# Re-timed loads, broadcasts and a gate pair in a Strassen-Winograd gated decoder block on one core

## The chip, the cores and the metric

The kernel runs on one core of one Trainium2 chip, in one launch. The metric is the device time of that launch in microseconds (us). Three runs before the change took 1220.03, 1220.82 and 1221.76 us; the median is 1220.82 us.

## The reference, cut to what matters

One decoder layer for 2048 tokens of width 1024, all in float32:

```python
c_act = silu(c)
shift, scale, gate = split(c_act @ w_ada + b_ada, 3)       # modulation
h = rms(x, g_pre) * (1 + scale) + shift
q, k, v, z_a, u_b, v_b, z_b, g = split(h @ w_in, ...)      # 4864 columns
q, k = rope(q, positions), rope(k, positions)              # 8 q heads, 2 k heads of 64
y_a = window_attention(q, k, v, sinks) * silu(z_a)         # blocks of 128
y_b = gelu(u_b) * (w_s @ layernorm(gelu(v_b)) + b_s) * silu(z_b)   # chunks of 128
merged = sigmoid(g_a) * (y_a @ w_proj_a) + sigmoid(g_b) * (y_b @ w_proj_b)
x = x + gate * rms(merged @ w_out, g_post)
```

## The kernel before, in words

**Products.** The large matrix products are Strassen-Winograd products: seven half-size products (p = 0 to 6) instead of eight. Both operands are split into a high and a low part, so one half-size product is twelve matmuls of 128x512: for each of four slices of the contraction, high by high, high by low (of the tokens) and low by high (of the weights), in `mm3` (L163, the matmul is on L168). The high part of a weight tile is a cast on ScalarE (L216), the low part a subtraction on VectorE (L217, shown as L151 W). The sums of weight quarters that Winograd needs (S1 to S4) are made in `combos` (L243), by VectorE for the first four column blocks and by GpSimd (L154) for the others, and are stored to `sS` for the second half of the tokens. The sums of the first four blocks stand in a list `sums`, which `sum_to` works off; the sum with index 4 to 7 is S1 of block 0 to 3, index 8 to 11 is S2 of block 0 to 3.

**Steps.** One step (`step`, L229) is one such product, twelve matmuls, 2.72 us from start to start where nothing waits. `slot` counts the steps. `later(n, f)` puts f ahead of the step n steps on, with `True` behind it. Every engine works through its own instructions in the order in which the program emits them; the order is written out by hand (`manual_schedule`), so an instruction that waits holds up all that stands behind it on its engine. DMAs go through SP's queue, but for a few.

**Stages.** The tokens are cut into two halves (s = 0, 1). Of the 38 column blocks of 128 of `w_in`, each Winograd block takes two: 19 blocks of seven steps, 133 steps for each half. The order of the blocks is the list `kinds` (L1255), matched by the column order in `_layout` (L1489). In the first half the first four blocks run interleaved: step 4p + i is product p of block i (steps 0 to 27). Step 28 is the first of the fifth block. While the steps go on, hooks do the rest: `rope_finish` (L881) turns q and k by the rotation tables (two DMAs, a multiplication on GpSimd, three operations on VectorE, a cast, two stores), `ln_step` transposes and normalises v_b, `att_block` does one of 16 attention blocks, eight steps apart, `ev_uz` the spatial gating, and `y_step`, `o_step` and `presum` make sums for later stages (GpSimd). After the two halves, `Pair` (L434) makes both projections of the first token half for two feature blocks at once, with eight PSUM banks, then come the second half and the output product.

**The start.** The token operand of product p (`T[p]`) is made on the fly in `t_part` (L748). It needs the modulation (`ada_row`, 16 matmuls for each of eight rows in all, then `ada_rows_out`, `ada_fin`) and the reciprocal root of each token's mean square (`rstd`, L643), which `rstd_out` (L653) broadcasts over the partitions with eight short matmuls and a copy. `rope_steps` makes the 24 VectorE operations on the angles, `rope_out` (L610) the sine and cosine tables, which go to DRAM (`cs_s`). `load_rope` (L798) loads them from there into four tiles of the pool `m` (four buffers, of which two hold results of the interleaved blocks up to steps 20 and 21) with four DMAs for each table.

**PSUM.** Four banks X, Y, Z, W are fixed, two (`s`) are the two halves of one tile S, two (`b`) are handed out by `bank()`.

Of the kernel before, what the change touches and what calls it, by code (L numbers as in the profile page):

```python
# [55 lines left out]
def hybrid_block(ctx: ExitStack, tc: tile.TileContext, xt, x, wada, wgate, wI, wP, wO,  # L56
# [286 lines left out]
    for n in range(NPAIR - NLAST):  # L343
        stream_fresh(wI_quads(n), n)
        if n == NFIRST - 1:
            by_product(NFIRST)
    for n in range(NPAIR - NLAST, NPAIR):
        stream_stored(wI_quads(n), n)
    by_product(NLAST)
# [268 lines left out]
    def rope_do(n):  # L618
        for _ in range(n):
            next(rope_it, None)  # L620
# [66 lines left out]
    def ada_rows_out(hf):  # L687
        rows[hf, "sb"] = flat("e")
        act.copy(rows[hf, "sb"], rows[hf])
# [84 lines left out]
    low_now()  # L774
    ada_load(1)
    cur["cap"] = 3 * NFIRST - 1
    ada_rows_out(0)
    warm(1, 2)
    ada_fin(0)
# [9 lines left out]
    want(NFIRST - 1)  # L789
    square_sums(1)  # L790
    low_now()
    rope_do(26)
    rope_out()


    ropet = {}

    def load_rope(s):  # L798
        for h in range(2):
            g = 2 * s + h  # L800
            for i, key in enumerate("cs"):
                t = flat("m")
                for r in range(4):
                    at = 64 * (r // 2) + r % 2
                    sp.dma_start(t[at : at + 64 : 2, :] if at < 64 else t[at:P:2, :], cs_s[i][32 * g : 32 * (g + 1), :])
                if key == "s":
                    later(3, lambda t=t: act.activation(out=t, in_=t, func=AF.Copy, scale=col[:, C_SGN : C_SGN + 1]))
                ropet[key, h] = t

    def setup_sgu():  # L810
        sp.dma_start(wT, ws)
# [101 lines left out]
    def ev_kv(s):  # L913
        def ev(key, src, psum):
            h = half(key)
            if ft(key) == 0:
                def put_out(hi, lo):
                    ks = slice(P + s * NT + h * 512, P + s * NT + (h + 1) * 512)
                    for i, t in enumerate((hi, lo)):
                        sp.dma_start(k_s[:, i, ks], t)  # L920
                rope_finish(h, rope_in(src, psum, "e"), put_out, (9, 3)[h] if s == 0 else h)
            else:
                t = src
                if psum:
                    t = flat("e")
                    act.copy(t, src)

                def turn():
                    b = bank()
                    for c in range(4):  # L930
                        pe.transpose(b[:, c * P : (c + 1) * P], t[:, c * P : (c + 1) * P], ident)

                    def out_():
                        o = flat("qS"[s])
                        act.copy(o, b)
                        at = 1 + s * 8 + h * 4
                        store(1, v_s[:, at : at + 4, :], o.rearrange("p (a b) -> p a b", a=4))
                    later(1, out_)
                later((3, 10)[h] if s == 0 else 2, turn, True)
        return ev  # L940

    def ev_q(s, g0):
        def ev(key, src, psum):
            h, g = half(key), g0 + ft(key)

            def put_out(hi, lo):
                for i, t in enumerate((hi, lo)):
                    sp.dma_start(q_s[s][:, i, g, h * 512 : (h + 1) * 512], t)
            rope_finish(h, rope_in(src, psum, "x"), put_out, ("11", "22", "12", "21").index(key))
        return ev  # L950

    def silu2(src, dst, psum, then=None):
# [297 lines left out]
    def run_all():  # L1250
        nonlocal T

        for s in range(NS):
            uz = [{} for _ in range(4)]
            kinds = [lambda: ev_vb(s, 0), lambda: ev_vb(s, 2), lambda: ev_kv(s), lambda: ev_g(s, 0), lambda: ev_q(s, 0),  # L1255
                     lambda: ev_q(s, 2), lambda: ev_za(s, 0), lambda: ev_za(s, 2)]
            kinds += [lambda c=c: ev_uz(s, c, uz[c]) for c in range(4)]
            kinds += [lambda j=j: ev_g(s, j) for j in range(1, 8)]

            if s == 0:  # L1260
                later(24, setup_sgu)
                later(28, zero_heads)
            later((23, 12)[s], lambda s=s: load_rope(s))
            for i in range(8):
                later((27 + 5 * i // 2, 17 + 3 * i)[s], lambda i=i: ln_step(s, i))
            for c in range(4):
                later(52 + 7 * c, lambda c=c: uz_load(s, c, uz[c]))
            for i in range(8):
                for off, post, f in att_block(s * 8 + i):
                    later(62 + 8 * i + off, f, post)  # L1270
            if s == 0:
                for i in range(8):
                    later(30 + 5 * i, lambda i=i: h1_stats(i))
                later(71, h1_rstd)
                for kt in range(4):
                    later(76 + 10 * kt, lambda kt=kt: h1_step(kt))
                for i in range(NLAST):
                    later(91 + 10 * i, lambda i=i: presum(NPAIR - NLAST + i, wI_quads(NPAIR - NLAST + i)))
            else:
                for i in range(4):  # L1280
                    later((1, 57, 64, 71)[i], lambda i=i: y_step((2, 3, 0, 1)[i]))
                for i in range(2):
                    later((78, 83)[i], lambda i=i: presum(NPAIR + i, p_quads(2 + i)))
                for kk in range(KT):
                    later(30 + 7 * kk, lambda kk=kk: gate_step(kk))
                for h in range(2):
                    later((91, 98)[h], lambda h=h: gate_end(h))
                for kt in range(4):
                    later(94 + 6 * kt, lambda kt=kt: o_step(kt))

            n0 = 0
            if s == 0:
                n0 = NFIRST
                S = pS.tile([P, 2, 512], F32, tag="s", name=nm("s"))
                bX = bank()
                rows["bank"] = bank()
                bks = [two_banks(BK["X"], BK["W"]), two_banks(BK["Y"], BK["Z"]), two_banks(S[:, 0, :], S[:, 1, :]),
                       two_banks(bX, rows["bank"])]
                blks = [Block(bks[i], kinds[i](), "mmee"[i]) for i in range(NFIRST)]

                def second_half():
                    ada_row(1, range(2))
                    rstd_out(1, BK["W"])
                    sum_to(2 * NFIRST - 1)
                    want(NFIRST)
                    ada_row(1, range(2, 8))
# [52 lines left out]
        S = pS.tile([P, 2, 512], F32, tag="s", name=nm("s"))  # L1359
        c = S[:, 0, :], S[:, 1, :], bank(), bank()  # L1360
        for n in range(2):
            blk = Pair(n, (BK, {"X": c[0], "W": c[1], "Y": c[2], "Z": c[3]}))
            for p in range(7):
                w = w_get()
                step(lambda: blk.run(p, w, T))
# [99 lines left out]
def _layout(inputs):  # L1465
# [26 lines left out]
    for j in range(1, KT):  # L1492
# [55 lines left out]
```

## Time and profile before

| | |
|---|---|
| median of three runs | 1220.82 us |
| the profiled execution | 1221.22 us |
| its span | 1219.5 us |
| mean granted TensorE clock | 0.993 |
| TensorE matmul (PE) busy | 1191.7 us, 98% of the span |
| VectorE (DVE) busy | 866.4 us, 71% |
| ScalarE (ACT) busy | 631.9 us, 52% |
| GpSimd (POOL) busy | 345.4 us, 28% |

A timeline row gives the start, the duration, the engine and line, the operation, what it writes and reads, the count of merged instructions, and in brackets the idle time of the engine ahead of it and what ended it. Rows of a merged group start where the group starts. SPq is SP's queue; its rows are the issuing of DMAs, not the transfers. In a list of waits the three numbers are the total in us, how often, and the longest.

### The profile page before, as it was taken

What the parts mean: (1) busy time and instruction counts of PE and PEld (TensorE: products, weight loads), DVE (VectorE), ACT (ScalarE), POOL (GpSimd) and SP (SyncE); (2) the same over time, 40 slices, a digit from 0 to 9 for tenths busy, and PEclk for the clock granted to TensorE, in tenths of its full rate; (3) what the DMA queues carried; (4) which work ended last, traced back from release to release, by engine and by line L of the source; (5) the groups of instructions that cost most, each with busy time, mean ns of one, the idle gap of its engine ahead of it and who ended that gap; (6) DMA issues with size and microseconds to landing.
All of it is one profiled execution on the core that took longest, in us unless ns stands there. A gap on an engine that the chain in (4) does not pass through costs nothing.

```text
span 1219.5 us, 17353 instructions
## 1 busy us (share of the span) xinstructions
PE 1191.7 (98%) x5450; PEld 951.1 (78%) x5450; DVE 866.4 (71%) x1319; ACT 631.9 (52%) x1367; POOL 345.4 (28%) x290
## 2 busy tenths in 40 slices
PE   8999899999999999999999999999999999999997
PEld 3677687888777777888878787777777888888886
DVE  7888589567868667346876877654786877767775
ACT  4475345475766677443445665555854512444443
POOL 0001365233456301011402122321033301155443
PEclk9999999999999999999999999999999999999999
DMA  9536888959899998578799899889967988855452
GB/s 350 219 121 204 280 296 294 279 167 220 261 353 349 311 298 301 180 228 273 244 282 294 252 258 327 275 266 283 340 217 240 384 275 266 286 170 172 139 182 87
DMA packets 227972, 311.74 MB, mean 256 GB/s; under 512 B 20900, under 2 KB 102948, under 8 KB 227880
## 3 DMA queue, kind: packets, MB, share of 16 engines
q1 hardware_dynamic: 227408, 309.94, 78.9%
q8 instruction: 43, 0.70, 0.2%
q0 software_dynamic: 176, 0.53, 0.2%
q14 instruction: 49, 0.40, 0.1%
q10 hardware_dynamic: 296, 0.16, 0.1%
HBM read 200.77 MB, written 104.53 MB: 250 GB/s over the span
## 4 chain that ended last, share of the span: by engine, by line
PE 89%; DVE 6%; ACT 2%; issue 2%; POOL 1%; DMA 0%; SPq 0%; DVEq 0%; POOLq 0%; ACTq 0%
PE bankY L168 28%; PE bankX L168 19%; PE bankZ L168 12%; PE bankW L168 12%; PE b L168 4%; PE s L168 4%; PE b L1095 2%; PE s L1045 2%; PE s L1046 1%; PE b L984 1%; DVE W L151 1%; PE b L1080 1%; PE b L683 1%; DVE e L157 1%; PE b L863 0%
## 5 line engine op out<-in xcount | busy, mean ns | idle before, releaser
L168 PE MATMUL bankY<-T,W 128*128 128x512 f32 x1578 | 386.1, 393 | 3.7 <-ACT bankY L432 1.6
L168 PEld LDWEIGHTS bankY<-T,W 128*128 128x128 f32 x1578 | 295.6, 189 | 66.2 <-issue 2.3
L151 DVE TENSOR_TENSOR W<-raw,W 128x512 fp32r<-128x512 f32 x327 | 270.1, 831 | 80.3 <-ACT W L216 79.7
L168 PE MATMUL bankX<-T,W 128*128 128x512 f32 x1110 | 272.5, 393 | 1.0 <-DVE T L745 1.0
L216 ACT CAST W<-raw 128x512 fp32r<-128x512 f32 x327 | 201.9, 618 | 127.3 <-PE b L168 40.9
L168 PEld LDWEIGHTS bankX<-T,W 128*128 128x128 f32 x1110 | 205.8, 188 | 45.4 <-DVE T L745 3.0
L168 PE MATMUL bankW<-T,W 128*128 128x512 f32 x684 | 169.9, 395 | 4.6 <-DVE W L151 2.9
L168 PE MATMUL bankZ<-T,W 128*128 128x512 f32 x684 | 166.4, 392 | 0.0
L168 PEld LDWEIGHTS bankW<-T,W 128*128 128x128 f32 x684 | 126.7, 189 | 34.4 <-DVE T L151 3.4
L168 PEld LDWEIGHTS bankZ<-T,W 128*128 128x128 f32 x684 | 128.4, 189 | 26.6
L154 POOL TENSOR_TENSOR S<-x,x 128x512 f32<-128x512 f32 x28 | 38.4, 1378 | 242.6 <-DMA x<-yb 101.7
L154 POOL TENSOR_TENSOR raw<-raw,raw 128x512 f32<-128x512 f32 x46 | 73.2, 1590 | 92.5 <-DVE W L151 31.4
L154 POOL TENSOR_TENSOR S<-raw,raw 128x512 f32<-128x512 f32 x23 | 37.5, 1630 | 152.3 <-DVE x L151 65.9
L151 DVE TENSOR_TENSOR T<-x,T 128x512 fp32r<-128x512 f32 (+1 forms) x105 | 72.6, 735 | 8.4 <-ACT T L384 8.3
L157 DVE TENSOR_TENSOR e<-bankY,e 128x512 f32<-128x512 f32 x43 | 29.6, 689 | 59.3 <-PE bankY L168 59.0
L168 PE MATMUL b<-T,W 128*128 128x512 f32 x270 | 66.4, 390 | 0.0
L168 PE MATMUL s<-T,W 128*128 128x512 f32 x258 | 63.5, 391 | 1.9 <-ACT b L493 1.9
L168 PEld LDWEIGHTS b<-T,W 128*128 128x128 f32 x270 | 50.9, 189 | 10.6
L168 PEld LDWEIGHTS s<-T,W 128*128 128x128 f32 x258 | 48.4, 188 | 12.4 <-ACT b L493 2.4
L384 ACT CAST T<-x 128x512 fp32r<-128x512 f32 x100 | 56.1, 619 | 2.4 <-PE s L168 2.1
L154 POOL TENSOR_TENSOR raw<-S,raw 128x512 f32<-128x512 f32 x23 | 34.0, 1479 | 76.2 <-DVE W L151 48.7
L1074 ACT ACTIVATE P<-P,rc 128x128 f32<-128x128 f32 x128 | 44.5, 396 | 12.5 <-DVE rc L1070 12.2
(270 smaller groups left out, 1422.6 us busy)
## 6 DMA issues: line engine op xcount, KB each, us to landing
raw<-in_wI SPq DMA_DIRECT2D x127, 256.0 KB, 4.6
raw<-sS SPq DMA_DIRECT2D x92, 256.0 KB, 5.0
g<-e SPq DMA_DIRECT2D x64, 256.0 KB, 4.0
sS<-raw SPq DMA_DIRECT2D x43, 256.0 KB, 4.5
T<-in_wada SPq DMA_DIRECT2D x16, 512.0 KB, 8.1
q<-q SPq DMA_DIRECT2D x64, 128.0 KB, 5.8
q<-k_s SPq DMA_DIRECT2D x64, 128.0 KB, 5.1
raw<-m SPq DMA_DIRECT2D x32, 256.0 KB, 4.6
```

The costliest lines, as they stand in the source:

```text
L151: dve.tensor_tensor(out=o, in0=a, in1=b, op=ALU.subtract)
L154: pool.tensor_tensor(out=o, in0=a, in1=b, op=op)
L157: dve.tensor_tensor(out=o, in0=a, in1=b, op=ALU.add)
L168: pe.matmul(o, w[:, i, sl], t[:, j, kt, :], start=start and kt == kts[0] and n == 0, stop=stop and kt == last and n == 2, skip_group_check ...
L216: act.copy(w[:, 0, :], src)
L384: act.copy(T[p][:, 0, kt, :], rs[kt])
L683: pe.matmul(rows[hf][64 * i : 64 * (i + 1), :], cact[:, kk : kk + 1].broadcast_to([P, 64]), adaw[hf][kk // 4][:, kk % 4, i * 512 : (i + 1) ...
L984: pe.matmul(b[:, ch * P : (ch + 1) * P], st["v", h][:, ch, :], wT[:, c, :], start=True, stop=True)
L1045: pe.matmul(o, q[:, g, :], k[:, 0, :], start=True, stop=False)
L1046: pe.matmul(o, q[:, g, :], k[:, 1, :], start=False, stop=True)
L1074: act.activation(out=st["P", kv][:, g, 0:P], in_=st["P", kv][:, g, 0:P], func=AF.Copy, scale=st["rc", kv][:, g : g + 1])
L1095: pe.matmul(o[own, :], v[:, k, own], st["pv", kv][k], start=k == 1, stop=k == 0)
```

## The change

- `rope_do(26)`, the last of the angle operations on VectorE, moves from ahead of the first step to ahead of `ada_rows_out(0)`; `rope_out` stays.
- In `second_half` (behind step 3) `rstd_out(1, ...)` comes ahead of all eight `ada_row(1, ...)` instead of behind the first two.
- S2 of blocks 0 and 1 joins the list entry 6 and so follows S1 of block 2 in `second_half`.
- `load_rope` loads the four tables at steps 12, 14, 22 and 24 of the first half instead of all at 23, and at 10 to 13 of the second instead of all at 12. The waits inside `rope_finish` become (6, 2) instead of (9, 3) for k in the first half, and at most 2 instead of 3 for q.
- `setup_sgu` moves from step 24 to 26 (its `go`, which takes a bank, from behind step 29 to behind step 31).
- The gate pair `ev_g(s, 1)` moves between the two q blocks: `kinds` and the columns of `w_in` are reordered. What follows is one block, seven steps, later: `uz_load`, `y_step` and `presum` by seven steps; attention by one; `gate_end` by three; `o_step` goes to steps 6, 98, 104, 110 from 94, 100, 106, 112.
- In the first two `Pair`s the second product uses the two halves of S as W and Z and the two `b` banks as X and Y; before, X and W lay in S.

```diff
+            for i in range(2):
+                sums[2 * NFIRST - 2].extend(sums[2 * NFIRST + i])
+                sums[2 * NFIRST + i] = []
...
+    rope_do(26)
     ada_rows_out(0)
...
-    rope_do(26)
     rope_out()
...
-    def load_rope(s):
+    def load_rope(s, ns):
+        def one(h, i, key):
+            g = 2 * s + h
+            t = flat("m")
+            for r in range(4):
+                at = 64 * (r // 2) + r % 2
+                sp.dma_start(t[at : at + 64 : 2, :] if at < 64 else t[at:P:2, :], cs_s[i][32 * g : 32 * (g + 1), :])
+            if key == "s":
+                later(3, lambda: act.activation(out=t, in_=t, func=AF.Copy, scale=col[:, C_SGN : C_SGN + 1]))
+            ropet[key, h] = t
         for h in range(2):
             for i, key in enumerate("cs"):
...
+                later(ns[2 * h + i], lambda h=h, i=i, key=key: one(h, i, key))
...
-                rope_finish(h, rope_in(src, psum, "e"), put_out, (9, 3)[h] if s == 0 else h)
+                rope_finish(h, rope_in(src, psum, "e"), put_out, (6, 2)[h] if s == 0 else h)
...
-            rope_finish(h, rope_in(src, psum, "x"), put_out, ("11", "22", "12", "21").index(key))
+            rope_finish(h, rope_in(src, psum, "x"), put_out, min(2, ("11", "22", "12", "21").index(key)))
...
-                     lambda: ev_q(s, 2), lambda: ev_za(s, 0), lambda: ev_za(s, 2)]
+                     lambda: ev_g(s, 1), lambda: ev_q(s, 2), lambda: ev_za(s, 0), lambda: ev_za(s, 2)]
...
-                later(24, setup_sgu)
+                later(26, setup_sgu)
...
-            later((23, 12)[s], lambda s=s: load_rope(s))
+            load_rope(s, ((12, 14, 22, 24), (10, 11, 12, 13))[s])
...
-                later(52 + 7 * c, lambda c=c: uz_load(s, c, uz[c]))
+                later(59 + 7 * c, lambda c=c: uz_load(s, c, uz[c]))
...
-                    later(62 + 8 * i + off, f, post)
+                    later(63 + 8 * i + off, f, post)
...
-                    later((1, 57, 64, 71)[i], lambda i=i: y_step((2, 3, 0, 1)[i]))
+                    later((1, 64, 71, 78)[i], lambda i=i: y_step((2, 3, 0, 1)[i]))
...
-                    later((78, 83)[i], lambda i=i: presum(NPAIR + i, p_quads(2 + i)))
+                    later((85, 90)[i], lambda i=i: presum(NPAIR + i, p_quads(2 + i)))
...
-                    later((91, 98)[h], lambda h=h: gate_end(h))
+                    later((94, 101)[h], lambda h=h: gate_end(h))
...
-                    later(94 + 6 * kt, lambda kt=kt: o_step(kt))
+                    later((6, 98, 104, 110)[kt], lambda kt=kt: o_step(kt))
...
-                    ada_row(1, range(2))
                     rstd_out(1, BK["W"])
+                    ada_row(1, range(8))
                     sum_to(2 * NFIRST - 1)
                     want(NFIRST)
-                    ada_row(1, range(2, 8))
...
-            blk = Pair(n, (BK, {"X": c[0], "W": c[1], "Y": c[2], "Z": c[3]}))
+            blk = Pair(n, (BK, {"W": c[0], "Z": c[1], "X": c[2], "Y": c[3]}))
...
-    cols = [wvb, wk, wv] + gates(0) + [wq, wza]
+    cols = [wvb, wk, wv] + gates(0) + [wq[:, 0:256]] + gates(1) + [wq[:, 256:512], wza]
```

More of the change, by code (lines that the diff above doesn't have):

```diff
@@ L791, in hybrid_block @@
     low_now()
-    rope_do(26)
     rope_out()
     ropet = {}
-    def load_rope(s):
+    def load_rope(s, ns):
[8 more added lines that the diff above has]
+            ropet[key, h] = t
         for h in range(2):
-            g = 2 * s + h
             for i, key in enumerate("cs"):
[L802 to L808, printed above, removed]
+                later(ns[2 * h + i], lambda h=h, i=i, key=key: one(h, i, key))
     def setup_sgu():
@@ L1255, in run_all @@
             kinds = [lambda: ev_vb(s, 0), lambda: ev_vb(s, 2), lambda: ev_kv(s), lambda: ev_g(s, 0), lambda: ev_q(s, 0),
-                     lambda: ev_q(s, 2), lambda: ev_za(s, 0), lambda: ev_za(s, 2)]
+                     lambda: ev_g(s, 1), lambda: ev_q(s, 2), lambda: ev_za(s, 0), lambda: ev_za(s, 2)]
             kinds += [lambda c=c: ev_uz(s, c, uz[c]) for c in range(4)]
-            kinds += [lambda j=j: ev_g(s, j) for j in range(1, 8)]
+            kinds += [lambda j=j: ev_g(s, j) for j in range(2, 8)]
             if s == 0:
-                later(24, setup_sgu)
+                later(26, setup_sgu)
                 later(28, zero_heads)
-            later((23, 12)[s], lambda s=s: load_rope(s))
+            load_rope(s, ((12, 14, 22, 24), (10, 11, 12, 13))[s])
             for i in range(8):
@@ L1487, in gates @@
         return [wg[:, j * P : (j + 1) * P], wg[:, D + j * P : D + (j + 1) * P]]
-    cols = [wvb, wk, wv] + gates(0) + [wq, wza]
+    cols = [wvb, wk, wv] + gates(0) + [wq[:, 0:256]] + gates(1) + [wq[:, 256:512], wza]
     for c in range(4):
         cols += [wu[:, c * P : (c + 1) * P], wzb[:, c * P : (c + 1) * P]]
-    for j in range(1, KT):
+    for j in range(2, KT):
         cols += gates(j)
```

## The prediction

> **What bounds the kernel now.** I read the page first, then TensorE's list of waits, then the timeline around each wait, because the page leaves little choice:
>
> ```profile
> span 1219.5 us, 17353 instructions
> ...
> PE 1191.7 (98%) x5450; PEld 951.1 (78%) x5450; DVE 866.4 (71%) x1319; ACT 631.9 (52%) x1367; POOL 345.4 (28%) x290
> ```
>
> TensorE's matmuls fill 98% of the span: 27.8 us of 1219.5 are idle, and some of that is the first microseconds and the tail behind the last matmul. The change takes no matmul out, so all it can win is idle time and the slow clock that follows idle time. GpSimd is idle for 72%. The list of waits names the idle time inside the stream:
>
> ```profile
> PE b L931 <- DVE Tt L825: 4.6, 1, 4.6
> ...
> PE bankW L168 <- DVE W L151: 2.9, 1, 2.9
> ...
> PE s L168 <- ACT b L493: 1.9, 1, 1.9
> ...
> PE bankY L168 <- DVE e L157: 1.6, 2, 0.8
> ```
>
> The 1.6 are two waits of 0.8, one in each token half. I set the sum up as a ledger of places, and for each I ask which instruction ends last there.
>
> **Place 1, steps 4 to 9 (45 to 75 us).** Timeline and one stretch of busy times (PE, PEld, DVE, ACT, POOL):
>
> ```profile
> 26.94 0.16 DVE L701 TENSOR_TENSOR AS<-b,col 128x4 f32<-128x4 f32 x1 [2.17 <-PE b L695]
> ...
> 39.30 0.42 DVE L557 TENSOR_SCALAR T<-T 128x512 f32<-128x512 f32 x1
> ...
> 40.94 0.43 DVE L557 TENSOR_SCALAR T<-T 128x512 f32<-128x512 f32 x1
> ...
> 42.20 1.02 POOL L148 TENSOR_TENSOR rs<-pw,nhalf 128x4 f32<-128x4 f32 x1
> ...
> 43.53 1.94 PE L683 MATMUL b<-T,cact 128*64 128x512 f32 x8
> ...
> 44.04 0.69 DVE L157 TENSOR_TENSOR S<-raw,x 128x512 f32<-128x512 f32 x1 [0.61 <-DMA x<-in_wI]
> ...
> 46.64 0.58 ACT L658 COPY e<-bankW 128x512 f32<-128x512 f32 x1 [4.55 <-PE bankW L655]
> ...
> 47.26 1.41 DVE L672 SCALAR_TENSOR_TENSOR q<-q,AS,e 128x512 f32<-128x512 f32 x2 [2.53 <-ACT e L658]
> ...
> 62.31 0.68 DVE L151 TENSOR_TENSOR P<-S,raw 128x512 f32<-128x512 f32 x1
> ...
> 67.42 0.68 DVE L151 TENSOR_TENSOR W<-P,W 128x512 fp32r<-128x512 f32 x1
> ...
> 68.16 3.50 PE L168 MATMUL bankW<-T,W 128*128 128x512 f32 x10 [2.88 <-DVE W L151]
> ...
> 71.47 3.62 PE L168 MATMUL bankZ<-T,W 128*128 128x512 f32 x12
> ...
> 74.92 2.88 PE L168 MATMUL s<-T,W 128*128 128x512 f32 x12
> ...
> 77.64 0.62 PE L168 MATMUL b<-T,W 128*128 128x512 f32 x2
> ```
>
> ```profile
> 47.30:67.40 20.10, 17.31 (x80) 11.43 (x76) 19.38 (x34) 10.70 (x18) 0.00 (x0) 1.00 0.06 19
> ```
>
> TensorE waits 2.88 us at step 8 for the low part of its weights (68.16), and VectorE, which makes it at 67.42, has been busy for 19.38 of the 20.10 us before. So VectorE's work from 47.26 on sets this place, and three edits pull at it.
> - The last four angle operations (39.30 the first, 40.94 the last, 1.98 us to the next instruction) move into a pause of 2.17 us ahead of 26.94. Cover: that pause. They fit with 0.2 us left; what they overrun delays step 0. I take 0, ends 0 and 0.5.
> - The broadcast no longer stands behind two of the modulation rows (43.53, eight matmuls, 1.86 us to the broadcast). The roots are ready at 43.22 (42.20 + 1.02), before TensorE reaches them, so no new wait; the copy at 46.64 comes at 44.8 and ends at 45.4. The rows themselves are only shifted: TensorE does the same work before step 4.
> - Two S2 (one is the 0.68 us at 62.31) move to behind the third S1 (44.04, over at 44.73): at 0.60 us from start to start VectorE is free at 45.9. Their two stores go to SP earlier by as much; SP has nothing there that step 4 to 8 needs.
>
> So the row at 47.26 starts at 45.9, 1.35 us earlier, and the stretch up to 67.42 loses one S2, 0.65. The other S2 stood behind 67.42 and does not count. The low part comes at 65.4, and step 8 goes on at 68.16 - 2.0 = 66.1. TensorE itself comes to it earlier as well (a 0.7 us wait at step 4 goes, with what followed), at some 63.9 instead of 65.28: a wait of 2.2 us stays. **Gain 2.0 us**, ends 1.0 (half the chain held by ScalarE's casts, which come in between) and 4.8 (the wait and its aftermath gone).
>
> The aftermath: 68.16 to 74.92 is 6.76 us for 22 matmuls that take 5.0 at the 2.72 us per twelve of an undisturbed step (74.92 to 77.64), so 1.77 us go to a slower clock. Does a wait of 2.2 us still cause it? In this trace 1.94 us (918.28 below) was followed by slow matmuls and 1.59 us (202.88) was not. I keep it. The Trainium skill, "TensorE: Matmul & The Clock Gate", Part 1 (The HAM clock gate), says that the clock halves only after an idle window of about 3.4 us; by that rule the step-8 wait would cost its 2.2 us alone and the total below would be 1.8 us lower. The 1.94 us row does not bear the threshold out; the price of a slow spell, 1.6 to 1.8 us in three places, agrees with half speed for one such window.
>
> **Place 2, steps 23 to 30 (110 to 142 us).**
>
> ```profile
> 109.99 10.08 SPq L805 DMA_DIRECT2D m<-cs  x16
> ...
> 128.87 0.59 ACT L926 COPY e<-s 128x512 f32<-128x512 f32 x1 [6.26 <-PE b L931]
> ...
> 129.87 0.60 ACT L971 ACTIVATE e<-b 128x512 f32<-128x512 f32 x1
> ...
> 131.45 1.02 PE L820 MATMUL b<-wT,ones 128*128 128x512 f32 x2
> ...
> 131.90 0.59 ACT L935 COPY q<-b 128x512 f32<-128x512 f32 x1
> ...
> 135.77 1.11 DVE L825 SCALAR_TENSOR_TENSOR Tt<-b,col,Tt 128x128 f32<-128x128 f32 x4
> ...
> 137.03 0.63 PE L931 MATMUL b<-cst,e 128*128 128x128 f32 x4 [4.56 <-DVE Tt L825]
> ...
> 137.41 4.58 PE L168 MATMUL bankY<-T,W 128*128 128x512 f32 x12
> ```
>
> SP issues sixteen table loads in one go, 10.08 us or 0.63 each. ScalarE sits 6.26 us for an `e` buffer until 128.87. Behind step 29 TensorE makes the column sums of `wT` (131.45), and then the transposes of v wait 4.56 us for the bank in which those sums lie, until VectorE has read them (135.77 to 136.9); the next step runs slow, 4.58 instead of 2.88. Loss 4.56 + 1.70 = 6.26. With `setup_sgu` at 26 the column sums come behind step 31, after both transposes, so these can't wait for them. What is late next: the other banks, read at 129.87 and 131.90 (over at 130.47 and 132.49, against TensorE's 131.45), so 0 to 1.1 us, and the copy that step 30 needs from ScalarE, which now has a cast and a sign multiplication (about 0.5 each) ahead of it. I take 1.0 left over. **Gain 5.3**, ends 6.3 and 0 (the wait comes back two steps on, a rival below).
>
> The table loads themselves: 4 x 0.63 = 2.5 us of SP at each of four places. At steps 22 and 24 SP first waits for the store that frees the `m` buffer, so SP is held about as long as before, but with stores and weight loads in between. Weights are fetched some eight steps, 22 us, ahead, which covers it; without that cover up to 2.5 us. 0.
>
> **Place 3, the q blocks (180 to 210 us, and about 611 us).** Busy times as above, then TensorE and SP:
>
> ```profile
> 180.00:206.00 26.00, 23.62 (x108) 18.93 (x107) 25.34 (x35) 11.63 (x23) 16.86 (x15) 1.00 0.88 306
> ```
>
> ```profile
> 202.88 3.01 PE L168 MATMUL bankY<-T,W 128*128 128x512 f32 x12 [1.59 <-ACT bankY L432]
> ...
> 209.16 3.03 PE L168 MATMUL bankY<-T,W 128*128 128x512 f32 x12 [0.55 <-ACT bankZ L432]
> ...
> 211.20 0.93 SPq L948 DMA_DIRECT2D q<-x  x2
> ```
>
> VectorE is busy 25.34 of 26 us, so the waits of 0.8, 1.59 and 0.55 us (2.9) are VectorE falling behind, ScalarE behind it. A gate pair needs one tanh and two additions of a kind that every block has, no rotation: between the q blocks it spreads eight rotations, three VectorE operations of 0.7 us or more each, over seven steps more. I take 0.9 as left: **gain 2.0** here, and 0.5 of the 0.8 in the second half; ends 0 and 3.7.
>
> What it puts in danger is the first attention block. The last q store now comes one step ahead of the loads that read it back, before it was six. Landing times (KB, us):
>
> ```profile
> q<-x SPq DMA_DIRECT2D x5, 256.0 KB, 4.0
> ...
> q<-q SPq DMA_DIRECT2D x4, 128.0 KB, 6.1
> ```
>
> From the put-out: 0.9 to issue, 4.0 to land, 2.5 for four loads, 6.1 to land, 13.5 us; the scores come five steps (13.6) and some short matmuls later, 14.4. The put-out of step 53 lagged its step by 2.0 us (211.20 against 209.16), so a wait of 1.1 us in the first half, near none in the second. **Loss 0.5**, ends 0 and 2.2.
>
> **Place 4, the second pair (914 to 924 us).**
>
> ```profile
> 916.12 1.14 ACT L216 CAST W<-raw 128x512 fp32r<-128x512 f32 x2 [7.64 <-POOL raw L154]
> ...
> 917.68 0.54 ACT L493 COPY b<-s 128x512 f32<-128x512 f32 x1
> ...
> 918.28 1.97 PE L168 MATMUL s<-T,W 128*128 128x512 f32 x6 [1.94 <-ACT b L493]
> ...
> 920.04 2.76 PE L168 MATMUL bankY<-T,W 128*128 128x512 f32 x6
> ...
> 922.61 1.66 PE L168 MATMUL b<-T,W 128*128 128x512 f32 x6
> ```
>
> The second product of the pair writes the half W of tile S and waits 1.94 us until ScalarE has read the half X of the same tile (917.68), which ScalarE did late because a cast ahead of it waited 7.64 us for GpSimd. Then the clock is slow: 918.28 to 920.04 and to 922.61 are 1.76 and 2.57 instead of 1.36. Loss 1.94 + 0.40 + 1.21 = 3.55. With X in a `b` bank W waits for nobody. Late next: the third product needs the copy at 917.68 minus one place, over by 917.8, and TensorE is there at 917.55, so 0.3 us stays. **Gain 3.3**, ends 2 and 3.6.
>
> **The rest**: attention, gating, gate and output sums shifted by one to seven steps, one `o_step` (four loads, four GpSimd subtractions, four stores) in steps 6 to 13 of the second half. They are covered by TensorE's stream, which shows no wait there, and by an idle GpSimd; without that cover some 4 x 1.6 us of GpSimd. The spatial gating now overlaps seven more steps of attention. I take **0.5 loss**, ends 0 and 3.
>
> **Sum**: 2.0 + 5.3 + 2.0 + 0.5 + 3.3 - 0.5 - 0.5 = 12.1 us off the profiled execution's 1221.2 us, which stands 0.4 above the median of 1220.8: 1208.7 us.
>
> **Rivals.**
> - *The bank wait comes back.* The transposes of `ln_step` stand right behind the column sums at step 31, and also want a bank. If they get the one with the sums, place 2 gives nothing and the pause moves two steps: 1208.7 + 5.3 = 1214.0. For it: before, the v transposes took that bank though the other was read at 132.49. Against: GpSimd and VectorE have less queued two steps later. Chance 0.20.
> - *Step 8 keeps its wait but not the slow clock*: 1208.7 - 1.8 = 1206.9. For: the wait is shorter than 2.88. Against: the 1.94 us row. The page of the Trainium skill named at place 1 would have it so. 0.10.
> - *All is recovered*: place 1 whole 4.8, place 2 whole 6.3, place 3 whole 3.7, place 4 3.6, no losses: 18.4, so 1202.4. For: every wait named has its cause removed. Against: VectorE at 19.38 of 20.10. 0.13.
> - *Slower: the late q pair.* If VectorE puts q out later than some 0.9 us behind step 59, every microsecond is TensorE's, in both halves, with 1.7 us of slow clock once it passes 1.9. To eat 12.1 us it needs a lag of some 5.5 us in both; at 8 it is 1208.7 - 0.5 + 2 x (7.1 + 1.7) = 1225.8. For: 25.34 of 26 busy. Against: lags of 2 us or less there now. 0.05.
> - *It does not do what it says*: places 1 and 2 unchanged, and new waits in attention eat 3 and 4, about 1220. 0.04.
>
> **Numbers.** The forecast has 0.48, 1204 to 1213 by itself. About 0.2%, 2.4 us, is what a measurement of this kernel can tell from no change. Faster: 0.48 + 0.20 + 0.10 + 0.13 = 0.91; within 0.2%: 0.04; slower: 0.05. From 1202 to 1215 leaves out the last two rivals and tails on either side, together under 2 in 10.
>
> **What the profile after would show.** Place 1: VectorE's first modulation of the second part some 1.3 us earlier, a wait at step 8 of 2 us. Place 2: no wait of the v transposes; a wait of TensorE for `Tt` at step 31 or 33 is the first rival. Place 3: VectorE below 90% in the q stretch; a wait of the first scores for a DMA is the fourth. Place 4: no wait for the copy by ScalarE. Wrong would be the forecast if the total of TensorE's idle time stays above 20 us, or if a new row over 3 us stands in its list of waits.

## The result, and the profile after

The changed kernel takes 1204.01 us in the median of four runs (1203.60 to 1204.96); the kernel before took 1221.29 beside it (1220.03 to 1224.04). The ratio is 0.9857, 95% interval 0.9838 to 0.9875. The profiled execution is that of 1204.96 us, 16.3 below the one of before.

The page after:

```profile
span 1203.2 us, 17372 instructions
...
PE 1186.6 (99%) x5450; PEld 949.4 (79%) x5450; DVE 867.2 (72%) x1319; ACT 640.4 (53%) x1375; POOL 348.1 (29%) x290
```

TensorE is now idle for 16.6 us instead of 27.8. Of its list of waits after (total, times, longest), what lies behind the first steps and is longer than 0.2 us:

```profile
PE bankW L168 <- DVE W L151: 2.0, 1, 2.0
PE bankW L168 <- DVE T L151: 1.8, 3, 0.8
...
PE s L1051 <- DMA q<-k_s: 0.8, 1, 0.8
```

The rows of 4.6, 1.9 and 1.6 us are gone, 2.9 has become 2.0, and one row is new (0.8 us for a load of `k_s`). For the ledger I compare when TensorE reaches the same step. First before: steps 0, 24, 25, 32 and 54 in TensorE's timeline, a wait in the second attention block that the prediction did not list, and the first product of the second pair (place 4). Then after: steps 0, 10, 24, 25, 32 and 54.

```profile
29.02 0.79 PE L168 MATMUL bankX<-T,W 128*128 128x512 f32 x1
...
113.00 1.75 PE L168 MATMUL bankW<-T,W 128*128 128x512 f32 x7
...
117.30 2.93 PE L168 MATMUL bankZ<-T,W 128*128 128x512 f32 x12
...
144.93 1.41 PE L168 MATMUL bankY<-T,W 128*128 128x512 f32 x5
...
212.03 0.84 PE L168 MATMUL bankZ<-T,W 128*128 128x512 f32 x3
...
265.74 0.39 PE L1045 MATMUL s<-q,q 128*128 128x256 f32 x1 [1.23 <-ACT P L1065]
...
914.82 1.52 PE L168 MATMUL bankW<-T,W 128*128 128x512 f32 x6
```

```profile
29.43 0.79 PE L168 MATMUL bankX<-T,W 128*128 128x512 f32 x1
...
73.16 2.20 PE L168 MATMUL s<-T,W 128*128 128x512 f32 x9
...
111.24 1.07 PE L168 MATMUL bankW<-T,W 128*128 128x512 f32 x4
...
116.61 2.91 PE L168 MATMUL bankZ<-T,W 128*128 128x512 f32 x12
...
137.86 2.33 PE L168 MATMUL bankY<-T,W 128*128 128x512 f32 x9
...
201.18 2.88 PE L168 MATMUL bankZ<-T,W 128*128 128x512 f32 x12
```

| stretch | before, us | after, us | difference |
|---|---|---|---|
| start to step 0 | 29.02 | 29.43 | +0.41 |
| steps 0 to 9 (place 1) | 45.90 | 43.73 | -2.17 |
| steps 10 to 23 | 38.08 | 38.08 | 0 |
| step 24 | 4.30 | 5.37 | +1.07 |
| steps 25 to 31 (place 2) | 27.63 | 21.25 | -6.38 |
| steps 32 to 53 (place 3) | 67.10 | 63.32 | -3.78 |
| step 54 to the end of the span | 1007.47 | 1002.02 | -5.45 |
| span | 1219.5 | 1203.2 | -16.3 |

The rows behind these differences, place by place (VectorE, ScalarE, SyncE and TensorE in the timeline after; the last fence is one stretch of busy times):

```profile
27.35 0.16 DVE L704 TENSOR_TENSOR AS<-b,col 128x4 f32<-128x4 f32 x1 [0.26 <-PE b L698]
...
46.12 1.41 DVE L675 SCALAR_TENSOR_TENSOR q<-q,AS,e 128x512 f32<-128x512 f32 x2
...
66.45 4.14 PE L168 MATMUL bankW<-T,W 128*128 128x512 f32 x10 [2.00 <-DVE W L151]
...
70.42 2.90 PE L168 MATMUL bankZ<-T,W 128*128 128x512 f32 x12
```

Place 1: the angle operations fill the pause ahead of 27.35 down to 0.26 us. The modulation starts at 46.12, which against step 0 is 1.55 us earlier than before. Step 8 waits 2.00 us, and ten matmuls take 3.97 us behind it instead of 2.27: the slow clock came this time (the granted clock is 0.50 from 67.00 to 70.41).

```profile
109.66 2.39 SPq L808 DMA_DIRECT2D m<-cs  x4
...
122.33 0.59 ACT L932 COPY e<-s 128x512 f32<-128x512 f32 x1 [1.66 <-issue]
...
136.64 1.02 PE L826 MATMUL b<-wT,ones 128*128 128x512 f32 x2
...
137.50 0.60 PE L869 MATMUL b<-cst,q 128*128 128x128 f32 x4
```

Place 2: SyncE's train of loads is 2.39 us long instead of 10.08, ScalarE waits 1.66 us for its copy instead of 6.26, and nothing waits before or behind the column sums (136.64).

```profile
170.00:196.00 26.00, 26.00 (x122) 21.48 (x121) 20.95 (x30) 12.74 (x28) 15.93 (x16) 1.00 0.94 327
```

Place 3: in the q stretch VectorE is busy 20.95 of 26 us instead of 25.34, and TensorE 26.00.

```profile
713.95 0.35 PE L1051 MATMUL s<-q,q 128*128 128x256 f32 x1 [0.75 <-DMA q<-k_s]
...
902.26 1.52 PE L168 MATMUL bankW<-T,W 128*128 128x512 f32 x6
...
906.75 1.55 PE L168 MATMUL b<-T,W 128*128 128x512 f32 x6
```

Place 4: from the first product of the second pair (902.26) to the fourth (906.75) it is 4.49 us; before it was 7.79 (914.82 above to 922.61 in the prediction's rows). The new wait, 0.75, stands ahead of the second scores of the third attention block of the second half; from the step ahead of them (708.45) to the one behind (714.98) it is 6.53 us, against 5.79 at the same place before (721.06 to 726.85).

Step 24 became longer, which nothing in the prediction foresaw. VectorE, GpSimd and TensorE after:

```profile
107.20 1.79 DVE L151 TENSOR_TENSOR T<-x,T 128x512 fp32r<-128x512 f32 x1
108.91 1.77 DVE L151 TENSOR_TENSOR W<-raw,W 128x512 fp32r<-128x512 f32 x1
110.61 1.77 DVE L151 TENSOR_TENSOR x<-x,wT 128x512 f32<-128x512 f32 x1
112.30 0.68 DVE L151 TENSOR_TENSOR T<-x,T 128x512 fp32r<-128x512 f32 x1
...
107.06 1.37 POOL L154 TENSOR_TENSOR S<-raw,raw 128x512 f32<-128x512 f32 x1 [63.85 <-DMA x<-e]
108.52 1.62 POOL L154 TENSOR_TENSOR raw<-raw,raw 128x512 f32<-128x512 f32 x1
110.09 1.74 POOL L154 TENSOR_TENSOR x<-x,m 128x512 f32<-128x512 f32 x1
...
114.84 0.96 PE L168 MATMUL bankW<-T,W 128*128 128x512 f32 x3 [0.83 <-DVE T L151]
```

Three VectorE operations with two inputs take 1.77 to 1.79 us while GpSimd runs; the fourth, with GpSimd done, takes 0.68. Before there were two long ones (1.79 and 1.78 us, at 109.57 and 111.28). The third is there because the multiplication of the k rotation (110.09) now stands directly behind the block sums.

### The profile page after: what moved, and what is told of

Its sections match the earlier page's. It is cut to its first block, busy times and chain, and to the rows that moved or that the text cites. A ratio compares the mean times of both kernels' runs of the same rounds, so it can differ in the third digit from the quotient of the medians.

```text
span 1203.2 us, 17372 instructions
## 1 busy us (share of the span) xinstructions
PE 1186.6 (99%) x5450; PEld 949.4 (79%) x5450; DVE 867.2 (72%) x1319; ACT 640.4 (53%) x1375; POOL 348.1 (29%) x290
## 4 chain that ended last, share of the span: by engine, by line
PE 88%; DVE 5%; DMA 2%; ACT 2%; issue 1%; SPq 1%; POOL 0%; DVEq 0%; ACTq 0%; POOLq 0%
PE bankY L168 27%; PE bankX L168 19%; PE bankW L168 12%; PE bankZ L168 12%; PE b L168 5%; PE s L168 4%; PE b L1101 2%; PE b L686 1%; PE s L1051 1%; PE s L1052 1%; PE b L1086 1%; PE b L990 1%; DVE W L151 1%; DVE e L157 1%; DMA e<-za 1%
## 5 line engine op out<-in xcount | busy, mean ns | idle before, releaser
L151 DVE TENSOR_TENSOR T<-x,T 128x512 fp32r<-128x512 f32 (+1 forms) x105 | 69.7, 711 | 3.5 <-ACT T L387 3.1
L168 PE MATMUL b<-T,W 128*128 128x512 f32 x282 | 69.3, 390 | 0.0
L168 PE MATMUL s<-T,W 128*128 128x512 f32 x246 | 60.0, 389 | 0.0
```

The costliest lines, as they stand in the source:

```text
L151: dve.tensor_tensor(out=o, in0=a, in1=b, op=ALU.subtract)
L168: pe.matmul(o, w[:, i, sl], t[:, j, kt, :], start=start and kt == kts[0] and n == 0, stop=stop and kt == last and n == 2, skip_group_check ...
```

## The experiments

Unless something else is said, times are from one profiled execution each, compared step by step, since the start up to step 0 alone varied from 28.98 to 30.43 us between executions.

### Place 2: the two steps or the table loads?

**e1_sgu24**, the changed kernel with

```diff
-                later(26, setup_sgu)
+                later(24, setup_sgu)
```

> The changed kernel with one number put back: setup_sgu is due at step 24 instead of 26. Theory (the two steps took away the wait of the v transposes and with it the slow clock): the wait of some 4.6 us for the bank with the column sums comes back between steps 29 and 31, with slow matmuls behind it, and the span is 5.3 to 6.4 us longer than that of the changed kernel. Rival (the table loads, now in four places, freed the engines around step 24, and the two steps did nothing): no wait, and a difference under 0.5 us.

1205.95 us. TensorE:

```profile
132.47 0.63 PE L937 MATMUL b<-cst,e 128*128 128x128 f32 x4 [1.31 <-DVE Tt L831]
```

Steps 25 to 31 take 22.73 us, 1.48 more than changed. Neither theory holds: the wait returns, but with 1.31 us and no slow clock. Seven tenths of the old wait were gone without the two steps.

**e2_sgu26**, the kernel before with

```diff
-                later(24, setup_sgu)
+                later(26, setup_sgu)
```

> The kernel before with one number changed: setup_sgu is due at step 26 instead of 24. Theory: the two steps are enough by themselves, the wait of 4.56 us and the slow clock behind it are gone, and the span is 5.3 to 6.4 us shorter than that of the kernel before. Rival (it needs the table loads out of the way too): the wait stays over 3 us and less than 2 us is gained.

1211.68 us, against 1218.83 of a run of before beside it. ScalarE and TensorE:

```profile
127.60 0.59 ACT L926 COPY e<-s 128x512 f32<-128x512 f32 x1 [6.26 <-PE b L931]
...
126.97 0.60 PE L931 MATMUL b<-cst,e 128*128 128x128 f32 x4
...
136.94 0.60 PE L863 MATMUL b<-cst,q 128*128 128x128 f32 x4
```

The transposes of 136.94 follow the column sums without a wait, and steps 25 to 31 take 21.26 us: by themselves the two steps win the whole 6.37. ScalarE is still stopped for 6.26 us, but nothing that TensorE needs hangs on it any more. Its row names the transposes of the other v tile, and the times agree: they end at 127.57, 0.03 us ahead of the copy, and before the change at 128.83 against 128.87. They read a tile of the pool `e`, of which the copy writes one. The last store out of `e` that SyncE issued ahead of the copy (`vb<-e`, at 125.20, before the change at 126.48) landed 4.4 and 3.5 us later, behind the copy in both kernels, so it is not what ScalarE waited for.

**e11_tables**, the kernel before with the table loads alone:

```diff
-            later((23, 12)[s], lambda s=s: load_rope(s))
+            load_rope(s, ((12, 14, 22, 24), (10, 11, 12, 13))[s])
```

> The kernel before with the table loads alone changed: four loads at each of steps 12, 14, 22 and 24 instead of sixteen at step 23, setup_sgu still at 24. Theory A (SyncE's 10.08 us train of sixteen loads held back the stores behind it, ScalarE waited 6.26 us for a buffer of theirs, and with it VectorE): ScalarE's wait at its copy of e from s falls below 2 us, the wait of the v transposes falls from 4.56 to some 1.3 us, as in the changed kernel with setup_sgu at 24, and the span is 3 to 5 us shorter than that of the kernel before. Theory B, the prediction's (the loads cost nothing, the wait is set by the step of setup_sgu alone): the wait stays over 4 us.

1214.32 us, against 1220.12 of before beside it. ScalarE and TensorE:

```profile
123.02 0.59 ACT L929 COPY e<-s 128x512 f32<-128x512 f32 x1 [1.66 <-PE s L168]
...
133.77 0.63 PE L934 MATMUL b<-cst,e 128*128 128x128 f32 x4 [1.31 <-DVE Tt L828]
```

Theory A's numbers come: without the train of sixteen loads ScalarE waits 1.66 us, and the v transposes 1.31 instead of 4.56, the same 1.31 as in e1_sgu24. Steps 25 to 31 take 22.77 us, 4.86 less than before. The theory's reason is not shown: ScalarE's copy is now released by the product in `s`, where before it was released by the transposes and not by a store of SyncE. Why the place of the loads changes what the copy waits for stays open. The two parts overlap: each by itself takes most of the 6.4 us, and beside the table loads the two steps are worth 1.48. The waits of place 3 stay in this run (1.56 and 0.81 us), so the table loads have no part in that gain.

### Place 4

**e3_pair**, the kernel before with the order of the banks alone:

```diff
-            blk = Pair(n, (BK, {"X": c[0], "W": c[1], "Y": c[2], "Z": c[3]}))
+            blk = Pair(n, (BK, {"W": c[0], "Z": c[1], "X": c[2], "Y": c[3]}))
```

> The kernel before with one part of the change: the banks of the second half's second q pair in the order of the change. Theory: the waits at that pair, 1.94 + 0.40 + 1.21 us, fall to some 0.3 us, and the span is 3.2 us shorter than that of the kernel before (3.0 to 3.6). Rival (part of that gain came from the gates' new places in the second half): under 2 us.

1216.68 us, 2.15 below the run of before beside it. TensorE:

```profile
914.03 1.52 PE L168 MATMUL bankW<-T,W 128*128 128x512 f32 x6
...
918.51 1.54 PE L168 MATMUL b<-T,W 128*128 128x512 f32 x6
```

The stretch is 4.48 us, 3.31 shorter than in the profile of before, and as long as in the changed kernel: the whole gain of place 4 is this line. But executions of the same code differ by the slow clock (below): in e2_sgu26 and e11_tables the pair still waited 1.93 and 1.94 us, no slow matmul followed, and the stretch took 6.30 and 6.31 us. Against those the line is worth 1.8 us, and 1.5 of the 3.31 are a slow clock that came in the profile of before.

### Place 3

**e5_nogate**, the changed kernel without the gate pair and with the steps that it shifts put back, all but those of `o_step`:

```diff
-                     lambda: ev_g(s, 1), lambda: ev_q(s, 2), lambda: ev_za(s, 0), lambda: ev_za(s, 2)]
+                     lambda: ev_q(s, 2), lambda: ev_za(s, 0), lambda: ev_za(s, 2)]
...
-    cols = [wvb, wk, wv] + gates(0) + [wq[:, 0:256]] + gates(1) + [wq[:, 256:512], wza]
+    cols = [wvb, wk, wv] + gates(0) + [wq, wza]
```

> The changed kernel without the gate pair between the q pairs: the gate block, its columns and the steps that were shifted by it are as before; everything else is as changed. Theory (the gate pair gave VectorE the time that it lacked in the q stretch): the three waits of before come back there, 0.79 + 1.59 + 0.55 us with the matmuls around them 3.8 us in all, and the one of 0.77 us in the second half, so 3.6 to 4.7 us longer than the changed kernel. Rival (the shorter delays of the rotations and the table loads at four places did it): no such waits, under 1 us longer.

1214.12 us. TensorE, and a row of its list of waits:

```profile
197.01 5.49 PE L168 MATMUL bankY<-T,W 128*128 128x512 f32 x12 [2.85 <-ACT bankY L435]
```

```profile
PE s L1051 <- ACT P L1071: 1.3, 1, 1.3
```

The theory's direction holds, its size does not: the span is 9.2 us longer, not 3.6 to 4.7. Of these, 7.1 lie in steps 32 to 53 (70.4 us, against 67.1 before). Most of what is above the forecast is the slow clock: it is 0.50 from 196.33 to 203.16 us, and the two steps behind the wait take 5.29 and 3.17 us instead of 2.72 each, 3.0 more. The waits are 0.81 and 2.85 us, where before had 0.79, 1.59 and 0.55. So without the gate pair the crowding is back, as before or a little worse. That one wait is now longer may come from the shorter delays of the rotations (6 and 2 for k, at most 2 for q); no run has them alone.

The wait of 1.3 us in attention also returns: it is in every profile without the gate pair and in none with it, so the gate pair with its shifted steps removed it. The new wait for `k_s` in the second half is not among this kernel's waits, but that shows little: a wait stands there, of 0.54 to 1.54 us, in seven profiles with the gate pair and in two others none does (e7_rows, e8_s2).

### Place 1

**e7_rows**, the changed kernel with

```diff
+                    ada_row(1, range(2))
                     rstd_out(1, BK["W"])
-                    ada_row(1, range(8))
                     sum_to(2 * NFIRST - 1)
                     want(NFIRST)
+                    ada_row(1, range(2, 8))
```

> The changed kernel with the first two modulation rows ahead of the broadcast again, as before. Theory: the broadcast's copy by ScalarE comes 1.35 us later against step 0, and the wait at step 8 is 2.9 to 3.4 us instead of 2.00. Rival (the moved block sums and angle steps made the 0.9 us, and the order of the rows costs nothing): 2.0 to 2.3 us.

1205.66 us.

```profile
68.59 2.56 PE L168 MATMUL bankW<-T,W 128*128 128x512 f32 x10 [2.29 <-DVE W L151]
```

The wait is 2.29, by the letter the rival's figure, but TensorE also reaches step 8 later: 35.67 us after step 0 (65.69 less 30.02) instead of 34.40. Steps 0 to 9 take 43.69 us, against 42.13 of the changed kernel in an execution without the slow clock (e1_sgu24). The order of the rows is worth 1.56 us; I had looked for all of it in one row.

**e8_s2**, the changed kernel without these lines:

```diff
-            for i in range(2):
-                sums[2 * NFIRST - 2].extend(sums[2 * NFIRST + i])
-                sums[2 * NFIRST + i] = []
```

> The changed kernel with the two S2 block sums left in their old places, behind the broadcast. Theory (each part of place 1 shows by itself: the order of the rows gave 1.56 us, the two sums 0.6 us): TensorE's wait at step 8 is 2.6 us instead of 2.00. Rival (the sums lie in a pause of VectorE in either place): 2.0 to 2.1 us.

1205.33 us.

```profile
67.61 4.11 PE L168 MATMUL bankW<-T,W 128*128 128x512 f32 x10 [2.60 <-DVE W L151]
```

As the theory has it: 2.60, the two sums are worth 0.60. Together with the rows that is 2.16 of the 2.17. No run puts the angle operations alone back, so whether the rows could have gained as much without their move is not shown.

**e6_low**, the changed kernel with one call more, which makes the low parts of step 8's weights earlier:

```diff
+                later(NFIRST + 1, low_now)
```

> The changed kernel with one call more: the low parts of step 8's weights are due ahead of the six T parts of the first part of the second half of the rows, not after the third. Theory: TensorE's wait of 2.00 us at step 8 falls below 0.5 us, and steps 8 to 10 take no longer than the others in any case: 2.0 us less from step 0 to step 10 against a run of the changed kernel without a slow clock there (the 1.7 us of slow clock come in some executions only: they followed the wait of 2.0 us in two runs of three), 3.7 against one with it. Rival (another product is late there as well, the T parts being now 1.3 us later): the wait moves to steps 9 to 12 and less than 0.7 us is gained.

1202.11 us. Step 8, and step 24 of the same execution:

```profile
63.78 2.90 PE L168 MATMUL bankW<-T,W 128*128 128x512 f32 x12
...
110.94 2.43 PE L168 MATMUL bankW<-T,W 128*128 128x512 f32 x5 [0.82 <-DVE T L151]
113.16 3.67 PE L168 MATMUL bankZ<-T,W 128*128 128x512 f32 x12
```

The wait is gone: steps 0 to 9 take 39.85 us, 2.28 less than without the slow clock and 3.88 less than with it. But at step 24 the clock is slow this time, behind waits of 0.73 and 0.82 us: steps 24 and 25 take 9.33 us instead of 8.12, which gives 1.21 back.

### Step 24

**e4_k93**, the changed kernel with

```diff
-                rope_finish(h, rope_in(src, psum, "e"), put_out, (6, 2)[h] if s == 0 else h)
+                rope_finish(h, rope_in(src, psum, "e"), put_out, (9, 3)[h] if s == 0 else h)
```

> The changed kernel with the k rotation's two finishing parts in the first half delayed by 9 and 3 steps instead of 6 and 2. Theory (step 24 lost 1.07 us because GpSimd's multiply of the rotation, 1.74 us, now runs next to the block sums and a third two-input VectorE operation takes 1.77 us instead of 0.68): step 24's operations at 110 to 112 us take 0.68 us again, its wait falls by about 1.07 us, and so does the span. Rival (the sums of the block themselves collide, whatever the rotation does): the step keeps its 5.37 us and the span does not change by more than 0.3 us.

1204.75 us. VectorE and TensorE:

```profile
110.14 1.77 DVE L151 TENSOR_TENSOR x<-x,wT 128x512 f32<-128x512 f32 x1
111.84 0.68 DVE L151 TENSOR_TENSOR T<-x,T 128x512 fp32r<-128x512 f32 x1
...
116.16 2.93 PE L168 MATMUL bankZ<-T,W 128*128 128x512 f32 x12
```

Step 24 takes 4.30 us (111.86 to 116.16), 1.07 less, and two long operations are left, beside the two block sums. The total did not show it: this execution came to step 0 at 30.00, 0.57 later.

### The clock behind a wait

In the profiled executions shown so far and below, TensorE waited behind step 0 fifteen times for 1.93 to 2.88 us. Behind eight of these waits the granted clock fell to 0.50, and the next matmuls cost some 1.7 us more (3.0 at place 3 in e5_nogate); behind seven it did not:

| wait, us | slow matmuls follow | none follow |
|---|---|---|
| 2.85 to 2.88 | before, e11_tables, e5_nogate (place 3) | e2_sgu26, e3_pair |
| 2.08 to 2.60 | e8_s2, e5_nogate (step 8) | e7_rows, after2 |
| 1.93 to 2.00 | after, e4_k93, before (place 4) | e1_sgu24, e2_sgu26 and e11_tables (place 4) |

Within these bounds the length does not decide. What does is where the wait falls. The granted clock changes on a fixed beat: in each of these traces the slow spells start whole multiples of 3.41 us apart and, ahead of the last microseconds, last 3.41 us or twice that (before: 69.52 to 72.93, 137.79 to 141.20, 919.44 to 922.85). Cut into pieces of 3.41 us on that beat, a trace shows how much of a wait fell into one piece. At the eight waits that were followed it is 1.94 to 2.60 us, and the next piece is slow; at the other seven the wait is split, and at most 1.88 us (1.21 to 1.88) fall into one. So the 2.00 us of after lie in one piece (63.59 to 67.00), and the 2.00 us of e1_sgu24 are split into 0.34 and 1.66 (at 65.78).

Three short waits at step 24 (0.7, 0.8, 0.2 us) were followed by slow matmuls in e6_low, e7_rows and after2, and not in four others. The first two wholly in one piece come to 1.52 to 1.57 us; that was followed in these three and not in after and e8_s2, so this case the rows alone do not settle.

### All repairs together

**after2** is the changed kernel itself, as the measure for the next two.

> The changed kernel as it is, once more, as the measure for the other kernels of this set on the same chip: 1204.0 us, at most 1 us to either side, since the slow clock behind the wait at step 8 comes in some executions only.

1205.41 us (1203.98 to 1205.96, four runs), in the upper part of what was expected. In its profile the wait in the third attention block of the second half is 1.54 us.

**e12_lowk** has the edits of e6_low and e4_k93.

> The changed kernel with the two repairs that showed a gain each: low parts of step 8's weights made earlier, and the k rotation's finishing parts delayed by 9 and 3 steps. Theory (they act at different places and add): 2.0 us at step 8, 1.07 us at step 24, and 0 to 1.7 us of slow clock, so 3.1 to 4.8 us less than the changed kernel, 1199.2 to 1201. Rival (with the earlier weights the block sums come earlier against VectorE's subtractions, and the slow clock turns up at step 24 instead): 2 to 3 us less.

1200.59 us (1199.76 to 1201.45), 4.8 below the changed kernel on the same chip; ratio to before 0.9833, interval 0.9814 to 0.9851. They add: in its profile steps 0 to 9 take 39.86 us and step 24 4.31, with no slow clock.

**e10_best** has these and

```diff
+        far = 3 if n == NFIRST else 1
-        plan = [(0, "A11", "raw"), (1, "A21", "raw"), (1, "A22", ("P", "P", "x", "x")[n] if first else "raw"),
+        plan = [(0, "A11", "raw"), (far, "A21", "raw"), (far, "A22", ("P", "P", "x", "x")[n] if first else "raw"),
```

> The same two repairs and a third: the loads of two of the four quadrant inputs of the first block of sums are issued two steps later, so that GpSimd's first two sums come after VectorE's subtractions of step 24. Theory (GpSimd beside VectorE makes those subtractions 1.77 us long instead of 0.68): TensorE's waits at step 24, 0.74 and 0.24 us, go too, 0.9 us less than with the two repairs. Rival (the weights of the steps behind then come late): a new wait at steps 25 to 28, and no gain or a loss against the two repairs.

1198.65 us (1198.39 to 1199.97); ratio to before 0.9819, interval 0.9800 to 0.9838. VectorE, GpSimd and TensorE:

```profile
105.16 0.69 DVE L151 TENSOR_TENSOR x<-x,wT 128x512 f32<-128x512 f32 x1
...
111.72 1.38 POOL L154 TENSOR_TENSOR S<-raw,raw 128x512 f32<-128x512 f32 x1 [67.73 <-ACT e L857]
...
107.99 2.88 PE L168 MATMUL bankW<-T,W 128*128 128x512 f32 x12
110.71 2.88 PE L168 MATMUL bankZ<-T,W 128*128 128x512 f32 x12
```

With GpSimd's sums some 8 us later against step 24 (104.27 in e12_lowk, where the step starts at 108.33) VectorE's operations are short, and step 24 takes 2.72 us like any other; it took 4.31 in e12_lowk. The gain is 1.6 us for waits of 0.77 and 0.24, so each wait cost some 0.3 us more than its row says. This is the fastest version: 5.4 us below the median of the changed kernel in its first runs, 6.8 below the one on the same chip.

## Why the prediction was right, and where it was not

The forecast was 1208.7 us with a range from 1202 to 1215; the time is 1204.0, at the edge of the likeliest case's own range (1204 to 1213) and nearer to the rival "all is recovered" (1202.4). The sign and the four places were right; the sum was 12.1 and the profiles differ by 16.3.

- **Place 1**: 2.0 forecast, 2.17 measured. The rows were put at 1.35 and the S2 at 0.65; the runs give 1.56 and 0.60 (the move of the angle operations was in the 1.35 too, and has no run of its own). The wait left was put at 2.2 and is 2.00. The angle operations cost step 0 nothing: from the last sums to step 0 it is 3.92 us in both kernels (25.10 to 29.02, 25.51 to 29.43), and the 0.41 us of the start arise ahead of them. The aftermath was kept, and it came, which was luck: it is missing in e1_sgu24 and after2, which have the same order there. A wait of 2.00 us is followed by it if at least some 1.9 fall into one piece of 3.41, an estimated chance of a little under one half ((3.41 - 2.00 + 2 x 0.1) / 3.41), so the term should have been half its size. The rival "step 8 keeps its wait but not the slow clock", which had 0.10, is true of some executions and not of others.
- **Place 2**: 5.3 forecast, 6.38 measured. The wait of the v transposes went as described. The step that failed is "the table loads themselves: 0": spreading them alone takes ScalarE's wait from 6.26 to 1.66 us and the transposes' from 4.56 to 1.31 (e11_tables). The cause is open; ScalarE's copy was released by transposes on TensorE, and with the loads spread it no longer waits for them. The sum hardly suffered, because the two parts take the same time twice. The 1.0 us left over did not appear. The first rival, that the wait returns at step 31, did not come; at step 24, with the loads spread, such a wait costs 1.5 us, not 5.3.
- **Place 3**: 2.0 + 0.5 forecast, 3.78 + 0.93 measured. Mis-sized twice. The waits of 0.79, 1.59 and 0.55 us were summed to 2.9, but by the starts of the steps they lost 1.09, 1.76 and 0.71; and I left 0.9 of them where nothing was left. The cause, that the gate pair gives VectorE room, is borne out by e5_nogate.
- **The first attention block**: 0.5 lost forecast, 0 measured: its first scores wait in neither half (228.38 and 642.48). So the fourth rival did not come either. The new wait for a load stands two blocks later in the second half and costs 0.74; what makes that load late I did not follow.
- **Place 4**: 3.3 forecast, 3.3 measured, and e3_pair gives it by that line alone. Of it 1.5 is the slow clock of one execution of before, which two others did not have; so the exact match is partly luck.
- **The rest**: 0.5 lost forecast. It holds a gain that the ledger lacked, the attention wait of 1.23 us (1.39 with the matmuls around it), and a loss that it lacked, 1.07 at step 24. I had moved the k rotation in time without looking at what runs on GpSimd and VectorE where it lands.

Of the 5.45 us behind step 54, place 4 has 3.30, attention 1.39, the second half's q wait 0.93, the new wait minus 0.74; 0.6 lie in pieces that I did not follow.

## What to carry to other kernels

Do not cost a train of DMAs at nothing because no row of TensorE names it: sixteen loads in one go, spread out by themselves, shortened the stops of two other engines by 4.6 and 3.25 us. Before a store is made the cause of a stop, compare when it landed with when the engine went on. Compare executions step by step and with the granted clock beside, since a wait of some 2 us costs its row or 1.7 us more by where it falls. When two edits act on the same wait, cost each alone and then together, since here each alone took three quarters or more of it. When a step is moved, look at the two engines that share something at the place where it lands, and add some 0.2 to 0.3 us to each wait of TensorE as its row states it.

## What the runs showed of the hardware that I had not expected

The slow clock after a wait is not a matter of the length alone: the same wait at step 8, 2.00 us, was followed at once (after), a step later in part (e4_k93: 0.97 and 0.81 us), and not at all (e1_sgu24). In these traces it is a matter of how much of the wait lies in one piece of a beat of 3.41 us: 1.94 us or more in eight waits of eight that were followed, at most 1.88 in seven of seven that were not. The Trainium skill, "TensorE: Matmul & The Clock Gate", Part 1 (The HAM clock gate), says that the activity window of about 3.4 us runs freely, so that the moment of a transition varies between runs; the runs agree with that, since the spells keep the beat within a trace and it lies differently against step 0 in each. They do not agree with the same section's rule that a whole idle window is needed: pieces in which TensorE was idle for 1.94 to 2.60 of the 3.41 us were enough.

A VectorE operation with two inputs takes 0.68 us alone and 1.77 to 1.79 beside a GpSimd operation with two inputs of 1.4 to 1.8 us; moving GpSimd away gave 0.69 (e10_best). The Trainium skill, "SBUF — State Buffer", section "SBUF: two separate sides", describes this as one port pair that the two engines lock in turn, the loser blocked for the other's whole instruction. The trace agrees: the three long operations of step 24 end at 108.99, 110.68 and 112.38, each 0.54 to 0.56 us after the end of a GpSimd operation (108.43, 110.14, 111.83), as if each had stood still until then.
